# A diffusion trunk layer on one NeuronCore: attention queries and keys computed feature-major in the seven-product stage, with their norm and rotation there

## The chip, the cores and the metric

The kernel runs on one core of a Trainium2 chip. The metric is the device time of one execution in microseconds (us); the median of three runs stands for it. A profile of one execution shows every instruction of the engines: PE (TensorE matmuls), PEld (its weight loads, which overlap PE), DVE (VectorE), ACT (ScalarE), POOL (GpSimd) and SP (SyncE, which here only issues DMAs). A line such as L54 is a line of the kernel; several helpers record every operation of one kind, so many groups carry the helper's line and are told apart by the names of their tiles.

## What is computed

One layer of a trunk over 640 tokens: 512 latent tokens of a sample and 128 context tokens of a prompt, 1024 features. A gated feed-forward half step, a token mixer and a second half step follow each other. The change is in the mixer, of which this matters:

```python
mq, mk, mv, mo, mg, dq, dk, dv, gm, gd = split_cols(h @ p['w_in'][l])
dq = rmsnorm(dq.reshape(B, T, DA_HEADS, 2, DA_HEAD_DIM), p['g_qn'][l])   # 8 heads, 2 x 64 features
dk = rmsnorm(dk.reshape(B, T, DA_HEADS, 2, DA_HEAD_DIM), p['g_kn'][l])
...
q_att = rope_2d(dq)                                  # latent tokens only
keys = jnp.concatenate([rope_2d(dk), k_ctx], axis=1)   # 512 + 256 cached; a prompt has its own 128
...
s = jnp.einsum('bqhcd,bkhcd->bhcqk', qi, kf) * scale
pr = jax.nn.softmax(s, axis=-1)
w = pr[:, :, 0] - lam * pr[:, :, 1]
return jnp.einsum('bhqk,bkhv->bqhv', w, vf)
...
y = jax.nn.sigmoid(gm) * (hm @ p['w_br_m'][l]) + jax.nn.sigmoid(gd) * (att @ p['w_br_d'][l])
```

`hm` comes from a chunkwise matrix memory (mLSTM) fed by mq, mk, mv, mg and gated by mo. The prompt's normed keys and its values are outputs too. In both streams modulation vectors, products of `c` with a wide matrix, scale and shift the activations.

## The kernel before

**Precision.** Each large product is made of three products in a fast 32-bit form: a weight and an activation are both split in a high and a low part, and high x high, high x low and low x high are added up in PSUM (`mm3`, L159; `mm`, L75). The split of a weight costs an ACT copy (high, L51) and a DVE subtraction (low, L54). Smaller products and turnings (`tr`, L78, a matmul with the identity) work on plain fp32.

**The seven-product form.** A product of 1024 x 256 weights (a *granule*) with 1024 x 640 activations is cut 2 x 2 x 2 and needs, by Winograd's scheme, seven block products in place of eight: `Winograd.products` (L383). A block product is 4 x 3 matmuls of 128 x 128 weights with 320 columns. The sums of weight blocks are made per granule by DVE and ACT (`Granule.parts`, L266, `sums`, L284), two granules ahead by the loads and one ahead by the splits. The products of a granule come in the order A11, S1, then the last two of the granule before, then S2, A12, S3; `between(i, 0)` and `between(i, 1)` are places in TensorE's order at a granule's start and after its A12. A quarter of the result is handed to `done(mt, hf, p, u)`, which copies it (ACT) or adds it to a kept part (DVE). The output is feature-major: features on partitions, tokens along the row.

**The mixer's stages.** (1) An opening in which pair 0 of the attention queries and keys is made token-major (`tok_group`, L1220), beside the second norm and the memory's gate product. (2) The *seven-product stage*, class `Gates` (L1914): twelve granules, six of the branch gates gd and gm, one of mq, one of mk and the four of mo, which pass a sigmoid. Each is stored to DRAM and fetched when it is needed. In `between` the first pair of queries and keys is normed and rotated, and seven *column tiles* of the modulation are made (`Columns.tile`, L805: two DVE products of 128 x 1024 with a sum along the row, L814). (3) *Attention*, eight heads of five blocks of 128 queries; four blocks are latent tokens with 768 keys, the fifth is the prompt with 128. (4) The memory, the branch products and the output.

**Attention.** Between the parts of a block stand *units* from a queue (`Fill`, L1245), in order: products that do not wait for the softmax. A *token unit* (`tok_unit`, L1211) makes 128 tokens x 256 columns with 24 matmuls of 256 columns, five to a granule; a *wide half unit* (`wide_units`, L1360) does two granules at once with 12 matmuls of 512 columns, ten to a pair; a *feature unit* (`feat_unit`, L1231) has 24 matmuls of 320 columns, four to a granule. The queue holds v0, k1, q1 and v1 as token granules, then five wide pairs (k2 with q2, v2 with mv0, k3 with q3, v3 with mv1, mv2 with mv3), then mq and mk of heads 1 to 3 and the last gates as feature granules. `UNITS` (L2097) says how many follow the softmax and how many the values in each block: two in some blocks, one in others, and three between two heads.

A block (L2101): `scores` puts 128 x 1536 scores of both components in three banks of PSUM that exist once, so the next block's scores wait until the exponentials have read them; a DVE minimum (queries carry a minus sign) is the exponent's bias; two ACT exponentials with sums along the row (`soft`, L1731); `mix` (L1739) joins the two components with lambda; in the next block, behind its scores, `turn` (L1747) transposes six pieces of 128 and `values` (L1759) multiplies them with the values. A head ends with a norm (`finish_norm`, L1769) and a transposition to feature-major (`finish`, L1778).

Queries and keys come token-major out of their units, so they are normed and rotated there in eight steps (`rope_steps`, L1530, four DVE passes over up to 1280 elements, dealt out by `rotate`, L1585); then a head's share is split and packed (`pack`, L1660) and turned to feature-major by TensorE: three packs of ten transposes (`turn_features`, L1679), evacuated by ACT and DVE.

**Order.** TensorE executes strictly in program order. ACT and DVE are ordered by a list scheduler, which takes an instruction when its inputs are ready by its own estimate, apart from what stands in `with written()`, which keeps the order of the code on each engine. `tc.issue_after(x)` keeps what follows behind x in that choice. SP and POOL issue their DMAs in order, and a DMA that must wait holds up those behind it. The memory's gate rows (`gate_rows`, L1428: two scans and some thirty small steps on DVE) run from attention's start into head 0; `gate_load` and `gate_cols` (L1509) need them in head 1.

## Time and profile before

| | us |
|---|---|
| median of three runs | 1806.32 |
| lowest, highest | 1805.69, 1807.44 |
| the profiled execution, device time | 1804.37 |
| its span, first to last instruction | 1802.4 |

The device time is the span and what lies around it. The granted TensorE clock was 1.0 throughout. The mixer's seven-product stage runs from 506.0 to 654.1 us of the span, attention from there to 1068.6.

```profile
PE   8999999999999999999999999999999999999998
...
DVE  6879887576888858777775637876768888896485
```

Each digit is the busy share of one fortieth of the span, in tenths. PE busy is the time in which a matmul is under way; matmuls overlap, so their start-to-start distance, not their mean duration, says what one more costs.

### The profile page before, as it was taken

To read this page: it belongs to the slowest core of one execution; us is meant where nothing else is said; L and a number is where in the kernel's file an instruction comes from. 1 tells how busy PE (TensorE), PEld (TensorE's weight loads), DVE (VectorE), ACT (ScalarE), POOL (GpSimd) and SP (SyncE) were. 2 spreads that over 40 slices of the span, in tenths; PEclk is the share of its full clock that TensorE was granted. 3 is DMA by queue.
4 is the path that set the end of the run, shared out by engine and by line. 5 is a ranking of instruction groups with operands and counts; after the bars stand their busy time and mean duration, and the time that the engine had idled before them with its cause. 6 is when DMAs were issued, how large, how long until landed. Compare 5 with 4: busy or idle time off the path is not lost.

```text
span 1802.4 us, 29657 instructions
## 1 busy us (share of the span) xinstructions
PE 1778.2 (99%) x11950; PEld 1712.3 (95%) x11950; DVE 1349.6 (75%) x2162; ACT 899.0 (50%) x1579; POOL 40.8 (2%) x72
## 2 busy tenths in 40 slices
PE   8999999999999999999999999999999999999998
PEld 6999999999999999888889998899999999999998
DVE  6879887576888858777775637876768888896485
ACT  5654544332655556565655546562326545544432
POOL 0000000100000000000000000000000000000010
PEclk9999999999999999999999999999999999999999
DMA  8364565978235543222222335665642455557992
GB/s 330 110 199 162 193 241 205 360 220 279 90 120 194 187 147 96 78 72 75 72 87 98 111 121 196 201 245 190 227 164 77 143 167 190 207 176 274 355 311 82
DMA packets 144923, 317.85 MB, mean 176 GB/s; under 512 B 10577, under 2 KB 106577, under 8 KB 133009
## 3 DMA queue, kind: packets, MB, share of 16 engines
q1 hardware_dynamic: 133410, 270.20, 43.7%
q0 software_dynamic: 10688, 43.13, 7.4%
q10 hardware_dynamic: 688, 2.63, 0.4%
q8 instruction: 94, 1.54, 0.3%
q14 instruction: 43, 0.35, 0.1%
HBM read 243.77 MB, written 72.15 MB: 175 GB/s over the span
## 4 chain that ended last, share of the span: by engine, by line
PE 85%; DVE 7%; DMA 4%; ACT 2%; issue 1%; SPq 0%; ACTq 0%; DVEq 0%
PE ps_f L75 48%; PE ps_p L75 15%; PE ps_t L75 10%; PE sc L75 3%; PE ps_o L75 2%; PE ps_n L75 2%; DVE ww L54 2%; DMA raw_a<-in_w_ada_k 1%; PE ps_wT L78 1%; PE ps_u L75 1%; PE ps_qkT L78 1%; DMA raw<-in_w2b 1%; DVE junk L814 1%; DMA a_raw<-aT_dram 1%; DMA P<-nm_dram 1%
## 5 line engine op out<-in xcount | busy, mean ns | idle before, releaser
L75 PE MATMUL ps_f<-S,ww 128*128 128x320 f32 x2400 | 387.2, 309 | 4.4 <-ACT u L51 1.9
L75 PEld LDWEIGHTS ps_f<-S,ww 128*128 128x128 f32 x2400 | 359.7, 188 | 8.7 <-DVE ww L54 4.6
L54 DVE TENSOR_TENSOR ww<-raw,ww 128x2048 fp32r<-128x2048 f32 (+1 forms) x73 | 163.9, 2245 | 66.0 <-ACT ww L51 65.9
L75 PE MATMUL ps_f<-hm,ww 128*128 128x320 f32 x1176 | 185.7, 309 | 0.1
L75 PEld LDWEIGHTS ps_f<-hm,ww 128*128 128x128 f32 x1176 | 175.7, 188 | 0.4 <-DVE ww L54 0.3
L51 ACT ACTIVATE ww<-raw 128x2048 fp32r<-128x2048 f32 (+1 forms) x73 | 136.8, 1875 | 59.7 <-DVE raw L54 40.3
L54 DVE TENSOR_TENSOR raw<-raw 128x1024 f32<-128x1024 f32 x186 | 160.8, 864 | 2.4
L75 PE MATMUL ps_f<-hm,wB 128*128 128x320 f32 x1008 | 161.5, 309 | 0.0
L75 PE MATMUL ps_t<-wH,hH 128*128 128x256 f32 (+1 forms) x440 | 151.6, 345 | 1.0 <-DVE x L57 0.9
L75 PE MATMUL ps_p<-hH,wH 128*128 128x320 f32 x480 | 150.9, 314 | 1.6 <-DVE num L54 1.6
L75 PEld LDWEIGHTS ps_f<-hm,wB 128*128 128x128 f32 x1008 | 151.3, 188 | 0.0
L75 PE MATMUL ps_p<-hH,wL 128*128 128x320 f32 x480 | 148.3, 309 | 0.0
L75 PE MATMUL ps_p<-hL,wH 128*128 128x320 f32 x480 | 148.3, 309 | 0.0
L75 PE MATMUL ps_t<-wH,hL 128*128 128x256 f32 (+1 forms) x440 | 146.4, 333 | 0.9 <-DVE hL L54 0.9
L75 PE MATMUL ps_t<-wL,hH 128*128 128x256 f32 (+1 forms) x440 | 146.3, 333 | 0.0
L51 ACT ACTIVATE u<-ps_f 128x320 f32<-128x320 f32 x129 | 55.7, 432 | 154.6 <-PE ps_f L75 154.5
L54 DVE TENSOR_TENSOR wL<-raw,wH 128x2048 fp32r<-128x2048 f32 x37 | 84.6, 2288 | 25.9 <-ACT wH L51 25.9
L51 ACT ACTIVATE wH<-raw 128x2048 fp32r<-128x2048 f32 (+1 forms) x45 | 75.4, 1681 | 49.7 <-PE ps_p L75 40.3
L54 DVE TENSOR_TENSOR wB<-raw,wB 128x1024 fp32r<-128x1024 f32 x64 | 78.0, 1219 | 26.6 <-ACT wB L51 26.6
L814 DVE CUSTOM_DVE_ANT_0 junk<-raw_a,csil 128x1024 bf16<-128x1024 f32 (+1 forms) x76 | 92.6, 1218 | 2.1 <-DMA raw_a<-in_w_ada_c 1.6
L75 PEld LDWEIGHTS ps_t<-wH,hL 128*128 128x128 f32 x440 | 83.6, 190 | 9.8 <-DVE hL L54 1.1
L75 PEld LDWEIGHTS ps_t<-wH,hH 128*128 128x128 f32 x440 | 83.5, 190 | 9.4 <-ACT nsq L51 1.1
(311 smaller groups left out, 3569.7 us busy)
## 6 DMA issues: line engine op xcount, KB each, us to landing
g_dram<-g SPq DMA_DIRECT2D x44, 640.0 KB, 7.5
raw_a<-in_w_ada_c POOLq DMA_DIRECT2D x38, 512.0 KB, 5.1
g_dram<-g SPq DMA_DIRECT2D x24, 480.0 KB, 8.6
raw<-in_w1b SPq DMA_DIRECT2D x11, 1024.0 KB, 4.9
raw<-in_w3b SPq DMA_DIRECT2D x11, 1024.0 KB, 6.4
raw<-in_w1a SPq DMA_DIRECT2D x10, 1024.0 KB, 4.9
raw<-in_w3a SPq DMA_DIRECT2D x10, 1024.0 KB, 6.2
hm<-g_dram SPq DMA_DIRECT2D x7, 1280.0 KB, 13.3
```

Of the source, the lines that this page charges most:

```text
L51: return placed(nc.scalar.activation(*args, **kw))
L54: return placed(eng.tensor_tensor(out=out, in0=in0, in1=in1, op=op))
L75: tc.keep_in_program_order(nc.tensor.matmul(*args, **kw))
L78: tc.keep_in_program_order(nc.tensor.transpose(*args, **kw))
L814: placed(vec.tensor_tensor_reduce(out=junk, in0=raw, in1=self.csil[:, v, :], op0=ALU.mult, op1=ALU.add, scale=1.0, scalar=0.0, accum_out=m ...
```

## The change

All eight granules of attention queries and keys move into the seven-product stage, ahead of, and in turn with, the eight gate, mq and mk granules; the four mo granules come last. The stage has twenty granules. The opening makes v0 and mv0 in place of q0 and k0, and stores them. In the queue of units stay mq1, (v1, mv1), mk1, (v2, mv2), (v3, mv3) and the feature granules as before: 62 units in place of 102.

```diff
+            turned = [(a[n], key, pr, None) for pr in range(4) for n, key in (("w_dk", 1), ("w_dq", 0))]
...
+            for src, dst, g, f in [w for two in zip(turned, plain) for w in two] + o:
```

A turned granule is feature-major as it arrives, in a tile `nat` of 128 x 2 x 640. Seven steps, one at each `between` from the granule after on, norm and rotate it there:

```diff
+        def squares():
+            nat = box["nat"]
+            box["sq"] = early.tile([128, 2, T], F32, tag="aux", name="sq", bufs=2)
+            act(box["sq"], nat, AF.Square)
         def sums():
+            sq = box.pop("sq")
+            for m in range(2):
+                for i in range(5):
+                    c = 2 * (5 * m + i)
+                    mm(p[:, c : c + 2], sq[:, m, i * 128 : (i + 1) * 128], halves[0], start=True, stop=True)
...
+            ts(v, p[:, 0:20], 1.0 / 64, ALU.mult, EPS, ALU.add)
+            act(t, v, AF.Ln)
+            at_rope[0] = act(y, t, AF.Exp, scale=-0.5)
+        def sine():
             newton_rsqrt(box["y"], box["v"], box["t"])
+            if not key:
+                ts(nrs[0][:, 2 * pr : 2 * pr + 2].rearrange("p m i c -> p (m i c)"), box["y"], -1.0, ALU.mult)
+            box["sw"] = sw = early.tile([128, 2, NS], F32, tag="sw", name="sw")
+            stt(sw, box["nat"][:, :, 0:NS], gs_, wide_table(tabs[1]), ALU.mult, ALU.mult)
+        def cosine():
+            nat = box["nat"]
+            if key:
+                tr(p[0:20, 0:128], box["y"], ident)
+                row = early.tile([20, 128], F32, tag="row", name="row", bufs=2)
+                act(row, p[0:20, 0:128], AF.Copy)
+                nc.gpsimd.dma_start(out=rk_dram[pr], in_=row)
+                box["rs"] = rs = early.tile([128, 2, T], F32, tag="aux", name="rs", bufs=2)
+                for c in range(2):
+                    nc.gpsimd.dma_start(
...
+            stt(nat[:, :, 0:NS], nat[:, :, 0:NS], g, wide_table(tabs[0]), ALU.mult, ALU.mult)
+            act(nat[:, :, NS:T], nat[:, :, NS:T], AF.Copy, scale=g)
+            sw = box.pop("sw")
+            for r in range(8):
+                o = r ^ 1
+                nc.gpsimd.dma_start(out=nat[16 * r : 16 * r + 16, :, 0:NS], in_=sw[16 * o : 16 * o + 16], accum_op=ALU.add)
+        def store():
+            nat = box["nat"]
+            if key:
+                tt(vec, nat, nat, box.pop("rs"), ALU.mult)
...
+            nc.gpsimd.dma_start(out=dst[2 * pr : 2 * pr + 2].rearrange("m p t -> p m t"), in_=nat)
+        def prompt():
+            if key:
+                for m in range(2):
+                    tr(p[:, 128 * m : 128 * m + 128], box["nat"][:, m, NS:T], ident)
...
+        return [squares, sums, sine, cosine, lambda: None, store, prompt]
```

The sums of squares over a head's 64 features, which now lie on partitions, are ten fp32 matmuls a granule with the squares as weights and two columns of ones and zeros. The partner of a feature in the rotation sits on another partition; its product with the sine is added by eight accumulating DMAs. Keys are multiplied by their roots, which go through DRAM to lie along the tokens. Queries are not: their roots, with the minus sign, stay in `nrs` and scale the exponent:

```diff
+            r = nrs[0][:, self.hd, qi]
+            stt(mn, mn, -1.0, r, ALU.mult, ALU.mult)
             for c, p in enumerate((p0, p1)):
-                self.exp = act(p[:, :w], sv[:, c, :], AF.Exp, bias=mn[:, c : c + 1], scale=-1.0, accum_out=sm[:, c : c + 1])
+                self.exp = act(p[:, :w], sv[:, c, :], AF.Exp, bias=mn[:, c : c + 1], scale=r[:, c : c + 1], accum_out=sm[:, c : c + 1])
```

The tables of cosine, sine and gains are turned once, by twelve transposes in the first granules. In attention a head is loaded from DRAM by five SP DMAs during the head before, and split in six steps, one at a time (`prepare`), three on ACT and three on DVE; packing, `turn_features` and the rotation go. Head 0 is split at the end of the seven-product stage.

```diff
+            return [queries, queries_low, lambda: keys(0), lambda: keys_low(0), lambda: keys(1), lambda: keys_low(1)]
```

The blocks of all heads follow each other without a place between heads, and the units are dealt anew; four units, not nine, come ahead of head 0. The seven column tiles of the seven-product stage go: five to head 7, two more to the d-branch (seven there in place of five).

```diff
-    UNITS = {hd: (two, one, two, one, one, (1, 1, 1)) for hd in range(7)}
-    UNITS[0] = (two, two, two, one, one, (1, 1, 1))
-    UNITS[7] = (two, one, two, one, (0, 0), (0, 0))
+    UNITS = {hd: (one, one, two, one, one) for hd in range(4)}
+    UNITS[4] = UNITS[5] = UNITS[6] = (one, one, one, one, one)
+    UNITS[7] = (one, one, one, one, (0, 0))
...
+        if hd == 7 and (qi, part) in ((0, 1), (1, 0), (1, 1), (2, 1), (4, 0)):
+            with written():
+                columns.tile()
```

## The prediction, made before the change was built or timed

> **What bounds the kernel now.** I read the page first, for the busy shares and the chain.

> ```profile
> span 1802.4 us, 29657 instructions
> PE 1778.2 (99%) x11950; PEld 1712.3 (95%) x11950; DVE 1349.6 (75%) x2162; ACT 899.0 (50%) x1579; POOL 40.8 (2%) x72
> ...
> PE 85%; DVE 7%; DMA 4%; ACT 2%; issue 1%; SPq 0%; ACTq 0%; DVEq 0%
> ```

> TensorE is busy for 99% of the span and holds 85% of the chain. So a change is worth the TensorE time that it removes, less the waits that it opens. Next the windows of the two stages that change, as busy time of PE, PEld, DVE, ACT, POOL, then clock and DMA: two granule pairs of the seven-product stage, and all of attention.

> ```profile
> 506.00:530.66 24.66, 24.66 (x171) 24.66 (x170) 18.80 (x29) 13.27 (x19) 0.00 (x0) 1.00 0.49 165
> 530.66:555.30 24.64, 24.64 (x170) 24.64 (x170) 21.87 (x29) 13.22 (x20) 0.00 (x0) 1.00 0.44 152
> ...
> 654.10:1068.60 414.50, 411.13 (x2736) 374.80 (x2735) 280.13 (x430) 230.81 (x483) 0.00 (x0) 1.00 0.27 86
> ```

> The seven-product stage has no TensorE gap, at full clock. Attention loses 414.50 - 411.13 = 3.4 us in 414.5. There is nothing to win from waits; only instructions can go. A matmul's own duration overlaps its neighbours', so I take the pitch from the chain of waits in order of time, where runs of one kind are merged (start, us, what, count).

> ```profile
> 41.58 0.39 PE ps_at L75 x4
> ...
> 506.02 148.09 PE ps_f L75 x1010
> ...
> 697.46 2.87 PE ps_t L75 x24
> ...
> 764.82 2.81 PE ps_t L75 x12
> ...
> 864.64 0.80 PE ps_qkT L78 x10
> ...
> 965.17 3.52 PE ps_p L75 x24
> ```

> A seven-product matmul takes 148.09 / 1010 = 0.1466 us, so a granule of 7 x 4 x 3 = 84 takes 12.3 us. A token unit 256 wide takes 2.87, a wide half unit (512) 2.81, a feature unit 3.52, ten turnings 0.80.

> **The TensorE sum.**
> - Added: eight granules (four of keys, four of queries), 8 x 84 x 0.1466 = **+98.5**.
> - Removed: four token granules of 256 columns (`v1` and `mv0` only swap places), 4 x 5 x 2.87 = **-57.4**; two wide pairs, 2 x 10 x 2.81 = **-56.2**.
> - Removed: turning, 8 heads x 3 packs of ten, 24 x 0.80 = **-19.2**.
> - Added: sums of squares. Ten fp32 matmuls per granule with two moving columns; the nearest row is `ps_at`, also two columns, where two such calls make four instructions in 0.39. So 8 x 20 x 0.0975 = **+15.6**. Bounds: the turning's pitch, 0.08 (12.8), and `ps_o`'s below, 0.112 (17.9).
> - Added: 12 turnings of tables, 4 of roots, 8 of prompt keys, at the 0.11 of `ps_wT` below: **+2.6**.

> Sum: 98.5 + 15.6 + 2.6 - 57.4 - 56.2 - 19.2 = **-16.1 us**.

> [...]

> **Waits in attention.** A block is scores, turn of the block before, one unit, values of the block before. Here is one (chain of waits) with a single unit ahead of it.

> ```profile
> 834.75 0.66 PE ps_wT L78 x6
> ...
> 848.71 1.41 PE sc L75 x8
> ...
> 850.14 1.77 DVE mn L1728
> ...
> 851.93 1.63 ACT p L51 x3
> ...
> 853.61 0.21 ACT p L51
> ...
> 854.04 0.23 DVE r L57
> ...
> 854.30 1.03 DVE p L57
> ...
> 855.37 0.87 PE ps_wT L78 x6
> ...
> 859.34 1.34 PE ps_o L75 x12
> 860.68 0.11 PE ps_wT L78
> ...
> 864.42 0.22 PE ps_o L75 x2
> ```

> The exponentials let go of the score banks 853.61 - 848.71 = 4.9 us after the scores begin; the mixed row is ready for the turn after 855.37 - 848.71 = 6.7. The change puts one more small DVE instruction between minimum and exponential, priced like `r`, 0.23: 5.1 and 6.9. TensorE's cover in an ordinary block is 1.41 + 0.66 + 2.81 + 1.34 = 6.2: enough. But heads now follow each other without the three units between them, and a head's first block turns and multiplies only the small prompt block: 1.41 + 0.11 + 2.81 + 0.22 = 4.55. The next scores wait 0.6 and the turn after them 0.3 more: 0.9 in the five heads whose first unit is a wide half, 0.25 in the three where it is a feature unit of 3.52. The fifth block waits some 0.2 at its turn, as at 855.37 now. I take **+7** (3 to 9). What hides the rest is the one unit per block; where it is missing, 2.8 more.

> Preparing a head moves off TensorE: three ACT and three DVE steps (two of 1024 and 1280 elements), each set behind the exponent's inputs, where DVE would wait 1.9 for the exponentials anyway; the whole rotation leaves DVE. I cost it at nothing. SP issues five small loads a head, next to the raw weights, which are fetched a granule ahead: nothing.

> **Head 0.** DVE rows of the timeline, the memory gates' rows:

> ```profile
> 671.31 1.47 DVE L1450 TENSOR_TENSOR_SCAN b<-keep,lf 4x640 f32<-4x640 f32 x1
> 672.81 1.48 DVE L1451 TENSOR_TENSOR_SCAN b<-keep,lf 4x640 f32<-4x640 f32 x1
> ...
> 676.60 0.81 DVE L54 TENSOR_TENSOR u<-ig,b 64x640 f32<-64x640 f32 x1
> ...
> 686.41 0.81 DVE L54 TENSOR_TENSOR ig<-fg,MP 64x640 f32<-64x640 f32 x1
> 687.15 1.74 DVE L1728 TENSOR_REDUCE mn<-sc 128x2 f32<-128x1536 f32 x1
> ```

> These rows take 2.95 + (687.2 - 676.6) = 13.6 us of DVE and end just ahead of the first minimum, 33 us after attention began. Nine units cover that now; afterwards four feature units, 14.1 us, and DVE has 4 us of head preparation in them too. Some 8 us of rows fall among the first blocks, where DVE is free for about 2 of 6.2. **+3** (0 to 8).

> **DVE in the seven-product stage and in head 7.** Groups of that stage by shape (count, busy, mean ns, idle before):

> ```profile
> L54 DVE TENSOR_TENSOR ww<-raw,ww 128x2048 fp32r<-128x2048 f32 x11 | 25.2, 2288 | 7.0 <-ACT ww L51 7.0
> L814 DVE CUSTOM_DVE_ANT_0 junk<-raw_a,csil 128x1024 bf16<-128x1024 f32 (+1 forms) x76 | 92.6, 1218 | 2.1 <-DMA raw_a<-in_w_ada_c 1.6
> L54 DVE TENSOR_TENSOR raw<-raw 128x512 f32<-128x512 f32 x22 | 15.2, 691 | 0.5
> L54 DVE TENSOR_TENSOR wB<-raw,wB 128x1024 fp32r<-128x1024 f32 x11 | 13.4, 1219 | 0.0
> L54 DVE TENSOR_TENSOR raw<-raw 128x1024 f32<-128x1024 f32 x11 | 13.4, 1216 | 0.0
> L54 DVE TENSOR_TENSOR g_out<-ps_f,u 128x320 f32<-128x320 f32 x20 | 9.7, 486 | 14.3 <-PE ps_f L75 14.3
> L54 DVE TENSOR_TENSOR wC<-raw,wC 128x512 fp32r<-128x512 f32 x10 | 6.8, 683 | 0.0
> ```

> A granule costs DVE 2.29 + 2 x 0.69 + 1.22 + 1.22 + 2 x 0.49 + 0.68 = 7.8 of 12.3. A turned one adds two products of 1024 elements (1.3 each, scaled from `p`, 1.03 for 768), small root steps (0.7) and for keys one product of 1280 (1.5): at most 4.8. A pair then holds 20.4 of 24.6, no more than the 21.87 that ran without a gap. ACT adds squares and copies, near 2.5, to 13.3 of 24.6. So throughput holds; latency is the question. TensorE runs in order and the sums wait for ACT's squares. The last quarter is ready after the fifth product of the next granule, 5 x 1.76 = 8.8, plus 0.5 and a square of about 1.3; TensorE arrives at 12.3. About 1.7 spare, behind which all of TensorE stands. **+1.5** (0 to 12).

> The seven column tiles leave this stage: two go to the d-branch, whose DVE has room:

> ```profile
> 1225.00:1281.00 56.00, 56.00 (x385) 56.00 (x384) 33.85 (x59) 15.32 (x16) 3.17 (x6) 1.00 0.65 232
> ```

> Five go to head 7, written into DVE's order between the blocks' steps, 2 x 1.22 = 2.4 each. Followed step by step on DVE (minimum 1.77 + 0.23, exponentials 1.9, mix 1.5, evacuation 0.35, tiles where written) head 7 ends its last mix near 36.5 us; TensorE's own sum is 5.25 + 3 x 6.9 + 0.6 + 2.4 = 29, and the end wait of about 1 is there today. **+6.5** (2 to 9). What would hide it is a second unit per block, and there is none.

> **Total.** -16.1 + 7 + 3 + 1.5 + 6.5 - 3.4 (today's waits, which these replace) = **-1.5 us**. The span would be 1800.9. The profiled execution took 1804.37, 2.0 over its span and 1.95 below the runs' median of 1806.32; set against the median the forecast is **1805**. 0.2% is 3.6 us, about what a measurement of this kernel can tell from no change.

> **Rivals.**
> 1. *The waits are hidden* (0.32). The scheduler fits gate rows and tiles into DVE's gaps, and only the block chain costs: -16.1 + 7 + 1.5 - 3.4 = -11: **1795**. For it: attention runs without gaps now at a DVE share of 280.13 / 414.5. Against: every block then has less cover than most have now.
> 2. *The accumulates come late* (0.20, slower). Rows of the DMA issues (KB, us to landing):

> ```profile
> x<-in_x POOLq DMA_DIRECT2D x4, 640.0 KB, 7.5
> P<-nm_dram SPq DMA_DIRECT2D x8, 320.0 KB, 6.1
> nm_dram<-fg SPq DMA_DIRECT2D x1, 160.0 KB, 2.4
> 561.97 2.28 DVE L54 TENSOR_TENSOR ww<-raw,ww 128x2048 fp32r<-128x2048 f32 x1
> ```

> POOL's queue holds nothing else in that stage, since the tiles' fetches leave it with them. For keys it stores the roots, waits, loads them back twice, then issues eight accumulates: by these rows up to 2.4 + 6.1 + 7.5 plus ten issues, some 20 us; all but the broadcasts move much less, so the least is about nothing over 12.3. One granule, 12.3 us, later DVE's multiply needs all of it. Queued behind it on DVE are the splits of coming weights, for which TensorE waits. Their margin: the split ending at 564.25 is first used at 506.02 + 5 x 12.34 + 1.76 = 569.5, 5 us. Past 12.3 + 5 = 17.4 us each of four key granules loses the excess; at 20 us 2.6 each, **1815**. [...]
> 3. *DVE sets attention's pace* (0.09): gate rows 8, tiles 9, chain 9: +8: **1813**.
> 4. *The sums are cheap* (0.03). [...]

> That the products are not saved cannot be: TensorE executes the listed matmuls. My forecast has 0.36.

> **Numbers.** Faster 0.35 (1 and 4), same 0.36, slower 0.29 (2 and 3). The forecast's own range is 1802 to 1809. Both signs hold much of the chance, so the range reaches from rival 1's 1794 to beyond rival 2, 1818.

> **What would show it.** TensorE busy falls by about 16 us whatever the time does. Stage by stage: the seven-product stage takes 148 + 98.7 + 18 = 265 us plus its waits, attention about 295. In the waits, `sc` behind ACT `p` and `ps_wT` behind DVE `p` near 17 us, half of it in heads 0 and 7. Wrong if the sums' matmuls start further apart than 0.11 or nearer than 0.08, if TensorE waits on `sq` or on a table, or if DVE waits on DMA in the seven-product stage (rival 2).

## The result: 4.4% slower, and the profile after

The changed kernel takes 1885.5 us (median of five runs, 1881.6 to 1885.5) where the kernel before takes 1806.3: a ratio of 1.0436, 95% interval 1.0421 to 1.0451. The forecast was 1805, the range 1794 to 1818. The profiled execution took 1885.5 with a span of 1883.7. From its page, the busy times, the clock row and the shares of the chain:

```profile
span 1883.7 us, 29739 instructions
PE 1797.5 (95%) x11846; PEld 1734.0 (92%) x11846; DVE 1359.2 (72%) x2208; ACT 906.6 (48%) x1561; POOL 109.4 (6%) x160
...
PE   8999999999999999978887989999999999999998
...
PEclk9999999999999999989998999999999999999999
...
PE 77%; DVE 11%; DMA 5%; ACT 4%; issue 2%; SPq 0%; DVEq 0%; ACTq 0%
```

TensorE has 104 instructions fewer and is busy 19 us longer; the clock row, all nines before, has eights; DVE has 11% of the chain. The chain of waits says how far the loss reaches. The first feed-forward run behind the mixer starts here, before and after:

```profile
1225.05 130.17 PE ps_p L75 x888
```

```profile
1305.99 130.17 PE ps_p L75 x888
```

Of the span's 81.3 us more, 80.9 arise ahead of it. Busy time, clock and DMA of each stage of the changed kernel (columns as in the prediction):

```profile
500.00:531.00 31.00, 27.66 (x176) 26.54 (x175) 21.14 (x29) 15.78 (x23) 0.00 (x0) 0.94 0.25 83
531.00:793.00 262.00, 255.52 (x1730) 253.14 (x1728) 157.74 (x198) 121.82 (x199) 68.57 (x88) 0.97 0.58 159
793.00:870.00 77.00, 57.69 (x323) 50.26 (x321) 54.21 (x91) 41.55 (x77) 0.00 (x0) 0.91 0.52 137
870.00:1147.00 277.00, 241.04 (x1454) 217.79 (x1454) 172.84 (x306) 138.12 (x288) 2.71 (x5) 0.92 0.36 105
1147.00:1305.99 158.99, 154.25 (x908) 141.36 (x907) 117.50 (x358) 97.87 (x251) 0.53 (x1) 0.99 0.61 205
sum 805.99, PE 736.17 PEld 689.09 DVE 523.42 ACT 415.14 POOL 71.81; mean PE 147.23 PEld 137.82 DVE 104.68 ACT 83.03 POOL 14.36
```

The same stretch before, as a sum over its three stages:

```profile
sum 725.05, PE 717.98 PEld 669.28 DVE 520.12 ACT 408.08 POOL 4.22; mean PE 239.33 PEld 223.09 DVE 173.37 ACT 136.03 POOL 1.41
```

TensorE stands for 805.99 - 736.17 = 69.8 us, before for 7.1. And it works at less than full clock. In stretches of 2 us, busy time x (1 - clock) adds up to 30.1 us lost, before to 0.0. What is left of the busy time, 736.17 - 30.1 = 706.1, is the work at full clock: 11.9 less than before. So +62.7 idle, +30.1 clock, -11.9 work: 80.9. The work was saved, and two things took it back several times over: waits, of which the prediction had priced 18 us, and the clock, which it had not priced. TensorE's waits by what ended them (us in total, times, longest):

```profile
PE ps_aT L78 <- DVE ao L54: 31.2, 7, 5.0
PE sc L75 <- ACT p L51: 16.9, 9, 10.8
PE ps_t L75 <- DVE wL L54: 3.1, 1, 3.1
...
PE ps_g L75 <- ACT sq L51: 2.1, 3, 0.7
PE ps_f L75 <- DVE ww L54: 1.8, 1, 1.8
```

The first row is new: seven of eight heads end with 3.6 to 5.0 us in which TensorE stands before the transposes of the finished head. The timeline of one such place:

```profile
862.28 0.35 DVE L61 TENSOR_SCALAR ao<-ps_o,rc 128x128 f32<-128x128 f32 x1
862.62 1.76 DVE L1674 TENSOR_REDUCE mn<-sc 128x2 f32<-128x1536 f32 x1
...
865.20 1.49 DVE L54 TENSOR_TENSOR qT<-qd,qT 64x1280 fp32r<-64x1280 f32 x1
865.20 0.99 ACT L51 ACTIVATE p<-sc,mn,nrs 128x768 f32<-128x768 f32 x1 [1.04 <-DVE mn L57]
...
867.15 1.05 ACT L51 ACTIVATE kH<-kd 128x1024 fp32r<-128x1024 f32 x1
...
869.72 0.82 DVE L54 TENSOR_TENSOR ao<-ao,ry 128x640 f32<-128x640 f32 x1
870.69 1.30 PE L78 MATMUL ps_aT<-ident,ao 128*128 128x128 f32 x5 [4.65 <-DVE ao L54]
871.79 2.77 PE L75 MATMUL ps_o<-v_tok,wT 128*128 128x128 f32 x12
```

The head's last values arrive at 862.6. Its norm is 3.5 us of small steps (square, sum, root, product), but they stand behind the next block's minimum, its exponentials and two steps of preparing the next head (`qT`, `kH`), and end at 870.5. TensorE, which comes there after one unit, waits 4.65 us. Behind the gap twelve matmuls of `ps_o` take 2.77; the prediction's row has 1.34 for them. The windows there show why (clock is the third number from the end):

```profile
866.00:870.00 4.00, 0.04 (x1) 0.00 (x0) 3.05 (x9) 3.05 (x9) 0.00 (x0) 0.94 0.42 118
870.00:872.00 2.00, 1.31 (x7) 1.34 (x7) 0.55 (x1) 0.19 (x1) 0.00 (x0) 0.50 0.65 156
872.00:874.00 2.00, 2.00 (x11) 2.00 (x11) 0.00 (x0) 0.76 (x2) 0.00 (x0) 0.50 0.19 74
874.00:876.00 2.00, 2.00 (x9) 1.81 (x9) 0.35 (x1) 0.00 (x0) 0.00 (x0) 0.50 0.30 96
876.00:878.00 2.00, 1.46 (x10) 1.10 (x8) 1.16 (x1) 0.72 (x2) 0.00 (x0) 0.92 0.57 157
```

Before the gap the clock is 1.00; it is halved 3.5 us into the gap and stays so for some 6 us of work.

### The profile page after: what moved, and what is told of

It is laid out like the page before. It is cut to its first block, busy times and chain, and to the rows that moved or that the text cites. A ratio compares the mean times of both kernels' runs of the same rounds, so it can differ in the third digit from the quotient of the medians.

```text
span 1883.7 us, 29739 instructions
## 1 busy us (share of the span) xinstructions
PE 1797.5 (95%) x11846; PEld 1734.0 (92%) x11846; DVE 1359.2 (72%) x2208; ACT 906.6 (48%) x1561; POOL 109.4 (6%) x160
## 4 chain that ended last, share of the span: by engine, by line
PE 77%; DVE 11%; DMA 5%; ACT 4%; issue 2%; SPq 0%; DVEq 0%; ACTq 0%
PE ps_f L75 51%; PE ps_p L75 12%; PE ps_t L75 3%; PE ps_o L75 2%; PE sc L75 2%; DVE ww L54 2%; DVE mn L1674 1%; PE ps_g L75 1%; PE ps_n L75 1%; DMA raw_a<-in_w_ada_k 1%; ACT p L51 1%; DVE junk L814 1%; PE ps_u L75 1%; DMA raw<-in_w2b 1%; PE ps_wT L78 1%
## 5 line engine op out<-in xcount | busy, mean ns | idle before, releaser
L75 PE MATMUL ps_f<-S,ww 128*128 128x320 f32 x2688 | 438.9, 312 | 5.6 <-DVE ww L54 2.1
L75 PEld LDWEIGHTS ps_f<-S,ww 128*128 128x128 f32 x2688 | 408.0, 190 | 10.4 <-DVE ww L54 6.6
L54 DVE TENSOR_TENSOR ww<-raw,ww 128x2048 fp32r<-128x2048 f32 (+1 forms) x81 | 182.3, 2250 | 139.0 <-ACT ww L51 138.9
L51 ACT ACTIVATE ww<-raw 128x2048 fp32r<-128x2048 f32 (+1 forms) x81 | 152.2, 1878 | 100.8 <-PE ps_f L75 53.8
L75 PE MATMUL ps_f<-hm,ww 128*128 128x320 f32 x1176 | 185.6, 309 | 0.1
L54 DVE TENSOR_TENSOR raw<-raw 128x512 f32<-128x512 f32 (+1 forms) x210 | 181.6, 865 | 2.6
L75 PEld LDWEIGHTS ps_f<-hm,ww 128*128 128x128 f32 x1176 | 175.7, 188 | 0.4 <-DVE ww L54 0.3
L75 PE MATMUL ps_f<-hm,wB 128*128 128x320 f32 x1008 | 161.5, 309 | 0.0
L75 PE MATMUL ps_p<-hH,wH 128*128 128x320 f32 x480 | 151.8, 316 | 3.5 <-ACT Cn L51 2.2
L75 PEld LDWEIGHTS ps_f<-hm,wB 128*128 128x128 f32 x1008 | 151.3, 188 | 0.0
L75 PE MATMUL ps_p<-hH,wL 128*128 128x320 f32 x480 | 149.0, 310 | 0.0
L75 PE MATMUL ps_p<-hL,wH 128*128 128x320 f32 x480 | 149.0, 310 | 0.0
L51 ACT ACTIVATE u<-ps_f 128x320 f32<-128x320 f32 x145 | 62.6, 432 | 156.0 <-PE ps_f L75 153.0
L54 DVE TENSOR_TENSOR wB<-raw,wB 128x1024 fp32r<-128x1024 f32 x72 | 87.9, 1220 | 36.0 <-ACT wB L51 36.0
L51 ACT ACTIVATE wB<-raw 128x1024 fp32r<-128x1024 f32 x72 | 75.7, 1051 | 44.1 <-PE ps_f L75 17.1
L75 PEld LDWEIGHTS ps_p<-hH,wH 128*128 128x128 f32 x480 | 90.8, 189 | 4.8 <-ACT Cn L51 2.6
L814 DVE CUSTOM_DVE_ANT_0 junk<-raw_a,csil 128x1024 bf16<-128x1024 f32 (+1 forms) x76 | 92.6, 1218 | 3.4 <-DMA raw_a<-in_w_ada_c 3.0
L75 PEld LDWEIGHTS ps_p<-hL,wH 128*128 128x128 f32 x480 | 90.8, 189 | 0.2
L75 PEld LDWEIGHTS ps_p<-hH,wL 128*128 128x128 f32 x480 | 90.7, 189 | 0.0
L75 PE MATMUL ps_f<-hm,wC 128*128 128x320 f32 x552 | 88.6, 309 | 0.1
L51 ACT ACTIVATE p<-sc,mn,nrs 128x768 f32<-128x768 f32 (+1 forms) x80 | 70.1, 882 | 32.4 <-DVE mn L57 32.4
L75 PEld LDWEIGHTS ps_f<-hm,wC 128*128 128x128 f32 x552 | 82.8, 188 | 0.4 <-DVE s L54 0.3
```

The costliest lines, as they stand in the source:

```text
L51: return placed(nc.scalar.activation(*args, **kw))
L54: return placed(eng.tensor_tensor(out=out, in0=in0, in1=in1, op=op))
L75: tc.keep_in_program_order(nc.tensor.matmul(*args, **kw))
L814: placed(vec.tensor_tensor_reduce(out=junk, in0=raw, in1=self.csil[:, v, :], op0=ALU.mult, op1=ALU.add, scale=1.0, scalar=0.0, accum_out=m ...
```

## The experiments

The theory is that the loss sits in separate places where TensorE stands (head ends, head 0, the stage's start, the rows of sums), each followed by half clock. The rival in each is that another engine is full there, and what is freed comes back at the next wait. Medians, each against the kernel before on the same chip:

| kernel | us | ratio, 95% interval |
|---|---|---|
| after | 1885.5 | 1.0436, 1.0421 to 1.0451 |
| e1_late | 1841.2 | 1.0203, 1.0188 to 1.0218 |
| e2_vplace | 1879.3 | 1.0413, 1.0393 to 1.0432 |
| e3_rows | 1878.9 | 1.0416, 1.0400 to 1.0431 |
| e4_sums | 1905.2 | 1.0572, 1.0544 to 1.0600 |
| e5_spread | 1880.7 | 1.0426, 1.0400 to 1.0453 |
| e6_rows2 | 1845.8 | 1.0217, 1.0201 to 1.0232 |
| e7_fill | 1877.1 | 1.0392, 1.0370 to 1.0414 |
| e8_best | 1827.9 | 1.0123, 1.0094 to 1.0153 |
| e9_tiles | 1843.7 | 1.0200, 1.0182 to 1.0217 |
| e10_queue | 1826.2 | 1.0105, 1.0090 to 1.0120 |
| e11_tables | 1821.1 | 1.0075, 1.0058 to 1.0092 |
| e12_last | 1814.0 | 1.0046, 1.0030 to 1.0062 |

The rows come from several chips, on which the kernel before took 1804.0 to 1806.3 us, so differences of a few us between rows are rough. The intervals of e2_vplace, e3_rows and e5_spread overlap with that of the changed kernel; what these edits did is read from their traces.

### Head ends: e1_late and e7_fill

```diff
-            if late is not None:
+            if late is not None and qi == 3:
                 late()
```

> One line differs from the kernel after: the transposes of a finished head's output (ps_aT) are issued in block 3 of the next head instead of block 1. Theory A (TensorE stands at ps_aT because the head's norm is worked off on ACT and DVE behind the next block's minimum and exponentials, and each gap of about 5 us halves the granted clock for the next 5 us): the seven waits of ps_aT, 31.2 us in all, go, and with them some 15 us of half clock: about 1840 us, the mean clock rises from 0.979 to about 0.987. Rival B (DVE and ACT are simply full at a head's start, so a wait moves to the next instruction that needs them): the waits reappear at sc or ps_wT, and the time falls by 10 us at most, 1875 or more.

44 us less, as theory A had it. `ps_aT` is gone from the waits, and the clock of the stretch with the head ends, 0.92 above, is 0.99:

```profile
870.00:1147.00 277.00, 266.01 (x1678) 238.87 (x1678) 199.26 (x397) 165.30 (x364) 2.72 (x5) 0.99 0.47 145
```

So the engines were not full; five transposes stood two blocks too early. The other run leaves the wait and fills the gap:

```diff
             if late is not None:
+                idle = psum.tile([128, 512], F32, tag="mm", name="ps_idle")
+                for k in range(18):
+                    mm(idle, H.kH[:, 0, 0:128], H.kH[:, 0, 0:512], start=True, stop=True)
                 late()
```

> On the kernel after: ahead of the transposes of each finished head 18 matmuls of 512 columns (fp32r, about 0.23 us each, 4.1 us in all), whose result nobody reads, are put into the gap in which TensorE stands there. Nothing waits for less. Theory A (the gap itself halves the clock): the gap is filled, the clock stays at 1.0 behind it, and some 2.5 us at six of seven head ends are saved, about 1870 us. Rival B (the low clock there has another cause, or the fill only delays the transposes): 1885 or more.

8.4 us less, half of what theory A had: with 126 idle matmuls more, the kernel is faster. From 870 to 1170 us the clock loss falls from 16.8 to 3.1 us, 13.7 less. The fill takes 7 x 4.1 = 29 us and covers 22 of idle time, so 7 of the 13.7 are given back. So the gap itself, not what follows it, halves the clock.

### The stage's start: e2_vplace

```diff
-            t = wide_p.tile([128, 512], F32, tag="CH", name="v_out", bufs=3)[:, 0:256]
+            t = ntmp.tile([128, HALF], F32, tag=("nsq", "nt")[i % 2], name="v_out", bufs=2)[:, 0:256]
```

> The first value tiles (v_out) are put in the two-buffer tiles of the later gate outputs (nsq, nt) instead of the buffers CH that the seven-product stage's weight halves wC use. Theory A (the first split of wC waits for the stores of v_out, the sums of raw weights and the split ww of the first granule come behind it, and TensorE stands 2.7 us at 506 to 510 and then runs at half clock): wC is split some 10 us earlier, the gap and about 2 us of half clock go: about 1880 us, 5 less. Rival B (the start is late because of the tables, which now come ahead of the first granules on ACT, DVE and SP): the gap stays, within 1 us of 1885.

6 us less by the medians, theory A. In the stage's trace (500 to 793 us) waits and clock loss fall from 18.3 to 13.1. ACT's splits of the first granule in the timeline, first after, then here:

```profile
499.30 1.15 ACT L51 ACTIVATE wC<-raw 128x512 fp32r<-128x512 f32 x2 [1.10 <-DMA v_dram<-v_out]
...
505.62 1.90 ACT L51 ACTIVATE ww<-raw 128x2048 fp32r<-128x2048 f32 x1
```

```profile
492.79 0.64 ACT L51 ACTIVATE wC<-raw 128x512 fp32r<-128x512 f32 x1 [0.81 <-DMA raw<-in_w_gd]
499.29 1.92 ACT L51 ACTIVATE ww<-raw 128x2048 fp32r<-128x2048 f32 x1
```

The value tiles had borrowed the buffers `CH` of the weight halves `wC`; their stores held `wC`, and `wC` held `ww`, for which TensorE stood.

### The sums: e4_sums and e5_spread

```diff
-        return [squares, sums, sine, cosine, lambda: None, store, prompt]
+        return [squares, lambda: None, sums, sine, cosine, lambda: None, store, prompt]
```

> An empty step is put between the squares and the sums of a turned granule, so that everything from the sums on comes half a granule later. Theory A (the half clock that follows three of the eight sums is set off by the 0.7 us in which the sums wait for the squares, on top of the 2.3 us of two-column matmuls): the waits on sq (2.1 us) and the three stretches of half clock (some 7 us of loss) go: about 1877 us. Rival B (the two-column matmuls alone count as idle for the clock): the waits go and half clock stays or comes at other granules: 1883.

20 us more, neither. Of the eight rows of sums one still waits, 0.3 us. Half clock comes behind four rows, three of them without any wait; here one of these, from 609.03 to 611.16 in the chain of waits:

```profile
609.00:611.00 2.00, 2.00 (x21) 2.00 (x20) 0.99 (x1) 1.30 (x2) 0.00 (x0) 1.00 1.04 267
611.00:613.00 2.00, 2.00 (x12) 2.00 (x12) 1.97 (x4) 0.44 (x2) 0.00 (x0) 0.75 0.98 377
613.00:615.00 2.00, 2.00 (x9) 2.00 (x9) 0.96 (x3) 0.44 (x1) 0.00 (x0) 0.50 0.28 106
```

TensorE is busy there throughout, by the profile. So a row of 20 two-column matmuls can halve the clock with no wait: rival B, though its 1883 is not the time. And another wait opened:

```profile
PE ps_g L78 <- DVE nat L54: 16.2, 4, 6.2
```

That is the prediction's second rival, at another place. DVE's product of the keys waits for the broadcast of the roots; in the second key granule the accumulates are issued from 626.2, the roots' store and broadcast behind them, and the product starts at 644.5, near the 20 us that the rival had worked out. But TensorE stands at the prompt keys' turnings, not for the splits of weights. In the changed kernel the product ends 4.3 to 9.1 us ahead of these turnings. The next run keeps all other places and breaks the row of sums in two (a hook behind each product issues ten of them):

```diff
+            def five(m):
+                for i in range(5):
+                    c = 2 * (5 * m + i)
+                    mm(p[:, c : c + 2], sq[:, m, i * 128 : (i + 1) * 128], halves[0], start=True, stop=True)
...
+            pieces.extend((lambda: five(0), lambda: five(1)))
...
-self.work.append([gr, lambda i: self.ops[i], done, lambda i: None])
+self.work.append([gr, lambda i: self.ops[i], done, lambda i: pieces.pop(0)() if pieces else None])
```

> On the kernel after: the 20 sums of a turned granule are no longer issued in one row at the granule's start but in two rows of ten, behind the next granule's first and second product; nothing else moves. Theory A (2.3 us of matmuls with two moving columns count as idle for the clock, which is why the run with the sums half a granule later still halved its clock behind every row of sums): with 1.76 us of full products between two rows of 1.1 us the clock stays, and the sums no longer wait for the squares: 8.5 us of clock less the start's 1.7, and 2 us of waits, so some 8 us less, 1877. Rival B (the roots come 2 products later and push the accumulates and the broadcast of the roots late, as they did when all steps moved): TensorE waits at the prompt keys' turnings, 1885 or more.

In the stage it did what theory A says: the clock from 531 us on is 1.00 where it was 0.97, the sums do not wait, and nothing waits at the prompt keys' turnings.

```profile
531.00:784.00 253.00, 249.09 (x1736) 247.72 (x1734) 158.97 (x199) 121.48 (x198) 68.66 (x88) 1.00 0.60 165
```

With the stage's start, from 500 us on, the clock loss goes from 8.5 to 1.7. The total fell by 5, less than theory A's 8, with runs from 1875 to 1888. Their mean clocks lie between 0.981 and 0.983, so the clock does not explain this range; it stays open.

### Head 0: e3_rows, e6_rows2, e8_best, e10_queue

```diff
-    ROWS = {(0, 0): 1, (1, 0): 1, (1, 1): 1, (2, 0): 2}
+    ROWS = {(0, 0): 1, (1, 0): 1, (2, 0): 1, (3, 0): 1, (4, 0): 1}
...
-                next(rows, None)
+                with written():
+                    next(rows, None)
...
-            if (hd, qi) == (0, 2):
+            if (hd, qi) == (0, 4):
                 begin_pools()
```

> The memory gates' rows are written into the order of the engines, one part in each of head 0's five blocks, behind the block's minimum and exponentials, and the pool that takes their room opens two blocks later. Theory A (the rows run on DVE ahead of head 0's first minimum, and TensorE waits 10.8 us at the second scores and 3.1 at the next weights, with about 4 us of half clock behind them): 12 to 18 us less, 1868 to 1873. Rival B (ACT and SP are late at that place anyway, since the store of a staged tile takes 9.2 us among the loads of two heads): TensorE still waits until about 815, 4 us less, 1881.

6.6 us less, between the two. In the changed kernel DVE had put all rows, 798.8 to 817.6, ahead of the first minimum. Now the longest wait at the scores is 3.8 in place of 10.8, but the chain then runs through a store:

```profile
807.45 0.46 ACT stage L51 x2
807.91 7.76 DMA mq_dram<-stage
...
815.78 0.34 ACT stage L51
...
816.50 2.06 ACT p L51 x4
```

ACT waits 7.8 us for one of two staging tiles, and head 0's exponentials are behind it.

```diff
-        if (qi, part) == (0, 0) and hd < 7:
+        if (qi, part) == ((0, 0) if hd else (1, 1)) and hd < 7:
             load_head(hd + 1)
```

> The later transposes of the first experiment and the written rows of the third, and besides the loads of head 1 move from head 0's first block to its second. Theory A (with the rows out of the way, head 0 waited for the store of a staged tile, 7.8 us in the DMA queues among the loads of head 1 and the raw weights): the wait at the second scores goes from 3.8 to about 1 and most of the half clock at head 0 with it; from 1841: 12 to 18 less, 1823 to 1829. Rival B (the stores are slow because of the raw weights and value tokens alone): as the sum of the two single experiments, 6 less than 1841, 1835.

1845.8, no better than the later transposes alone; theory A fell, but not on its merits: the planner (the list scheduler) still issued the loads ahead of the stores, so the edit changed nothing on SP. Head 0 gained 2 us; from head 6 on the run lost 5 to waits and half clock, 3 of them in heads 6 and 7. Why there is open. The five edits together:

> All five edits that leave the work as it is: transposes of a finished head in the next head's block 3, v_out in other buffers, the rows written into head 0's blocks, head 1's loads a block later, and the sums in two rows. Theory A (the losses are separate places on TensorE's path and add up): 1885 - 44 - 6 - 16 - 8, about 1811 us, still above the kernel before, since about 8 us of score and turn waits in the blocks, head 7's tiles and the wait for the query and key loads of memory remain. Rival B (one engine's total, DVE's or ACT's, is the bound behind them): 1830 or more.

1827.9, between the two and near rival B's 1830. The gains measured one by one (44 + 6 + 7 + 5 = 62) add up to most of the 58 gained here; the 16 us that theory A counted on at head 0 did not come. The stores on another queue, on top of that (`nc.sync` to `nc.gpsimd` for the stores of mq, mk and v):

> The five edits together (1828 us), and the stores of the staged tiles of memory's queries, keys and values are issued on POOL's queue instead of SP's. Theory A (in head 0 the scores wait for ACT, which waits 7 to 10 us for a staged tile's store behind the loads in SP's queue): the store takes about 3 us, the gaps of 4.0 and 3.8 us at head 0's first two blocks and some 4 us of half clock go, 8 to 11 less: about 1818. Rival B (the store is slow because all DMA engines are busy at 0.85 there, whatever the queue): 1828.

1826.2, no clear change. The store took 5.6 us in place of 9.2 (medians), but ACT still waited 8.5 for a staging tile, where it had waited 9.0, and the wait at the scores stayed at 4.0.

### Head 7's tiles and the tables: e9_tiles, e11_tables

```diff
-        if hd == 7 and (qi, part) in ((0, 1), (1, 0), (1, 1), (2, 1), (4, 0)):
-            with written():
-                columns.tile()
```

> The first experiment (transposes of a finished head in the next head's block 3, 1841 us) with head 7's five column tiles taken out of its blocks; they run after attention instead. Theory A (the tiles cost about what the prediction said, 6.5 us, of which the trace of the first experiment shows 4 us of TensorE gaps in head 7): 1834 to 1837. Rival B (the tiles are hidden, or cost as much after attention, since DVE prepares the memory stage there): 1841 or more.

1843.7 against 1841.2, no gain. But the edit does not do what it was meant to do. Outside `written()`, the scheduler still ran the ten products of the five tiles at 1049.8 to 1074.0 us, just ahead of head 7 and in its first blocks (its first scores are at 1055.3). One of them stands between two links of the block chain, and TensorE waits:

```profile
1057.74 0.21 DVE L57 SCALAR_TENSOR_TENSOR r<-sm,nlam,rc 128x1 f32<-128x1 f32 x1
1057.88 1.21 DVE L814 CUSTOM_DVE_ANT_0 junk<-raw_a,csil 128x1024 bf16<-128x1024 f32 x1
...
1059.02 0.34 DVE L57 SCALAR_TENSOR_TENSOR p<-p,r,p 128x128 f32<-128x128 f32 x1
...
1059.51 0.30 PE L78 MATMUL ps_wT<-ident,p 128*128 128x128 f32 x1 [2.53 <-DVE p L57]
```

In e1_late, where the tiles are written into the blocks, no wait at `sc` or `ps_wT` in head 7 is over 1.8. So neither theory was tested, and what the tiles cost alone stays open.

```diff
-slots = {(0, 1): [lambda: turn_tables(0)], (1, 0): [lambda: turn_tables(1)], (1, 1): [lambda: turn_tables(2)]}
+slots = {(0, 1): [lambda: turn_tables(0)], (1, 1): [lambda: turn_tables(1)], (2, 0): [lambda: turn_tables(2)]}
...
+            if key:
+                pieces.append(row)
```

> The five edits together (1828 us), and two moves in the seven-product stage: the second and third turning of the tables come a step later each, and a key granule's turning of its roots comes one product later. Theory A (TensorE waits 2.0 us there for a table's copy, with 1.7 us of half clock behind it, and 3.0 us in four waits for the roots): 5 to 7 less, about 1822. Rival B (the later roots make the broadcast of the roots late, and DVE and then TensorE wait for it at the prompt keys): 1828 or more.

1821.1, 7 less, theory A. (`row` is the turning, the store and the broadcast of a key granule's roots, one product later.)

### All of it: e12_last

Head 1's loads carry a dependence on the last store of mq, and `UNITS` of heads 0 to 3 is `(two, one, one, one, one)`.

> The seven edits so far (1821 us) and two more: head 1's five loads are bound behind the last store of memory's queries on SP (in the runs before, the planner still issued them ahead of these stores, although they stood a block later in the program), and the second unit that heads 0 to 3 had in their third block moves to the first block, where only the small prompt block is turned. Theory A (head 0's scores wait for ACT, and ACT for stores behind these loads; the first block of a head lacks one unit of cover): the waits of 6.4 and 3.3 us at head 0 with their half clock go to about 3, and some 1 us in each of three heads: 10 to 13 less, 1808 to 1811. Rival B (the stores are held up by the 1 MB of raw weights, which still go first): only the cover helps, 3 less, 1818. Both are still above the kernel before, since heads 5 to 7 keep about 8 us of waits.

1814.0, between the two. The issues of the store (KB, us to landing), in e11_tables and here:

```profile
mq_dram<-stage SPq DMA_DIRECT2D x4, 160.0 KB, 10.8
```

```profile
mq_dram<-stage SPq DMA_DIRECT2D x4, 160.0 KB, 1.8
```

So the loads were what held the stores. The longest wait at head 0's scores, 6.4 us in e11_tables, is 0.5. The sum of the windows from 500 us to the feed-forward run, and the two largest groups of waits:

```profile
sum 730.91, PE 706.35 PEld 663.18 DVE 521.07 ACT 411.49 POOL 72.00; mean PE 141.27 PEld 132.64 DVE 104.21 ACT 82.30 POOL 14.40
```

```profile
PE sc L75 <- ACT p L51: 8.4, 9, 1.8
PE ps_wT L78 <- DVE p L57: 6.4, 7, 2.0
```

The clock is 1.00 in each of these windows. Idle time is 24.6 us, 17.5 more than before; work is 11.6 less; together +5.9 in the profiled execution, where the medians differ by 7.7. Of the six executions the profiled one is the shortest; the others have mean clocks of 0.996 to 0.998. No version tried beats the kernel before. Nine edits took back 71 of the 79 us.

## Why the prediction was wrong, step by step

**The head's end, the step that failed.** "What hides the rest is the one unit per block" was worked out for scores, turn and values, and not for `finish_norm` and `finish`. Before, two units and two turnings of keys lay between these, and then the next head's first block up to its values. The change puts the norm behind one block's values and the transposes one block later. The prediction counted the three lost units as cover of the next scores (+0.9) but not as the norm's, whose DVE and ACT steps now stand behind the next minimum and exponentials. With the head's preparation "at nothing", two of its steps were put into that queue too. Measured: 31.2 us of waits, 44 with the clock, by e1_late.

**The clock, a term that was not there.** The prediction read its rows "at full clock" and let no wait change that. Half clock cost 30.1 us in all; at the head ends e7_fill shows that the gaps cause it (16.8 us lost from 870 to 1170 us, 3.1 with the gaps filled). It was a rival that the prediction left out, although the longer waits that it allowed for (up to 8 us at head 0) were subject to it. Nor does it take an empty TensorE: the gap of 4.65 us above halved the clock, but so did two stretches of 3.41 us in the same trace in which TensorE was busy for 0.46 and 0.48 (last section).

**Head 0: +3 (0 to 8), measured some 17.** Two waits (10.8, 3.1) and 3.2 us of half clock. "Some 8 us of rows fall among the first blocks, where DVE is free" was wrong: the planner put all rows ahead of the first minimum. And SP's loads "nothing" was wrong here: head 1's held the stores, 10.8 us (e11_tables) against 1.8 (e12_last).

**The seven-product stage: +1.5 (0 to 12), measured 18 in 293 us** (500 to 793: 9.8 idle, 8.5 clock). "About 1.7 spare" for the sums was wrong. TensorE came to them some 12.3 us after the granule's start, as forecast, but in three of eight granules the last quarter's sum had stood behind a split of weights on DVE (2.29 us), and the square behind a split and a copy on ACT; TensorE waited 0.7 us each time, 2.1 in all. The rest were terms not in the sum: the buffers `CH` (5 to 6 us by e2_vplace), roots and tables (7 by e11_tables), the clock behind the rows of sums (e5_spread).

**The work: -16.1, measured -11.9 and -11.6.** The sign and most of the size held. A row of sums that does not wait takes 2.13 us in the chain (the prediction: 1.95), 1.4 more over eight; the other 3 are not accounted for. No run shows cheap sums (rival 4): 2.13 us for 20 matmuls is 0.107 each, above `ps_at`'s 0.0975.

**Right:** the block chain. In the changed kernel `sc` behind `p` and `ps_wT` behind `p` hold 6.7 us in heads 1 to 6, for a term of +7. With the other causes gone (e12_last, which deals some units anew) they hold 14.8: 4.7 there, 3.3 in head 0 (+3 was forecast) and 6.8 in head 7 (+6.5), where "near 17 us, half of it in heads 0 and 7" was said. Before, they were 2.6 in all.

**Rivals.** The accumulates do not decide here: DVE waited for the roots' broadcast once, 3.5 us, the sign that the prediction had named, and TensorE not at all. In e4_sums, half a granule later, they do. That head 7's waits are those of its tiles no run shows. DVE did not set attention's pace: e1_late gained 44 us with DVE's work unchanged.

## What to carry to other kernels

When units of cover are taken from a loop, list every chain that they covered, the rare ones at a head's end too, and for each ask what now stands ahead of it on the engines that work it off. Price a long wait of TensorE with the half clock behind it: in the changed kernel 2.3 to 2.8 us more for each of six gaps of 4.05 to 5.03. A moved load or a borrowed buffer is free only if nothing in its queue, and no later owner of the buffer, waits for what it displaces: here a store behind moved loads landed after 10.8 us, without them ahead of it after 1.8, and the borrowed buffers cost 5 to 6 (e11_tables, e12_last, e2_vplace).

## What the runs showed of the hardware

All figures of this section are counts in the traces of this case, from windows of 2 us (the clock) and of 3.41 us (busy shares) and from timelines and chains (gaps and rows).

- Of the gaps of TensorE in six traces (after, e1, e8, e9, e10, e12, from 500 us to 1160 or 1180), all 13 of 3.79 us or more were followed by half clock, and 11 of 22 between 1.75 and 3.6. This one of 3.55 us, in the changed kernel, kept the clock (the windows next to it show 1.00).

```profile
1072.62 0.76 PE L78 MATMUL ps_aT<-ident,ao 128*128 128x128 f32 x5 [3.55 <-DVE ao L54]
```
